# One decoder layer on one core: the opening's modulation rows asked for one block sooner, and the last head's scores and outputs as three float32r products each

## The chip, the cores and the metric

The kernel runs on one core of one Trainium2 chip. The core has five engines with an instruction stream each: TensorE (PE, matrix products; its weight loads are listed as PEld), VectorE (DVE), ScalarE (ACT), GpSimd (POOL) and SyncE (SP), which here only issues transfers between HBM and the on-chip memory SBUF. Matrix products are written into PSUM. The metric is the device time of one execution in microseconds (us); less is better.

## The reference

The reference is one layer of a decoder with 512 positions and a width of 1024, all in float32. A conditioning vector `c` gives six rows of 1024 numbers, the modulation, which scale, shift and gate the two halves of the layer.

```
mod = silu(c) @ ada_w + ada_b                  # 6 rows: sh1, sc1, g1, sh2, sc2, g2
u   = rms_norm(x, mix_pre_g) * (1 + sc1) + sh1
proj = u @ w_in                                # q, k, v, o gate, i/f gates, glu
q, k = silu(causal depthwise conv, width 4)
h   = mlstm(q, k, v, i, f)                     # 4 heads x 256, see below
y   = silu(layer_norm(causal depthwise conv, width 31, of a * sigmoid(gt)))
x   = x + g1 * rms_norm(concat(h, y) @ w_out, mix_post_g)
u   = rms_norm(x, ffn_pre_g) * (1 + sc2) + sh2
a, gt = causal depthwise conv, width 3, of u @ ffn_up
x   = x + g2 * rms_norm((silu(gt) * a) @ ffn_down, ffn_post_g)
```

For each of the four heads the mLSTM amounts to a causal attention without softmax: the scores q·k are multiplied by an exponential weight of the gates, E, and the result is multiplied with v. One more column of ones beside v gives the divisor. The head's output is normalised, gated and goes through `w_out` with the convolution group.

## The kernel before

**Number types.** A float32 product on PE is issued as two instructions. For its large products the kernel uses float32r, a shorter type, and makes up for it by splitting each operand into a high part (the rounded value, written by ACT) and a low part (what is left, subtracted on POOL or DVE). `mm3` (L207) then issues three products, high x high, high x low and low x high, into the same PSUM bank. `w_split` (L185) makes both parts of a weight tile; `w_load` (L195) loads and splits. The attention of all four heads is in plain float32.

**Order.** PE and SP issue in the order in which the text traces the instructions. Within the block `in_order()` (L76) the same holds for DVE, ACT and POOL; elsewhere a scheduler places their instructions when the kernel is built, earlier text first. `behind(ins, anchor)` fixes that one instruction comes after another on its engine. A tile from a pool with n buffers waits until the tile that last had its buffer has been read for good; `slots` has 36 buffers of 128x512 numbers, from which most temporary tiles come. SP is one queue: an issue that waits holds up all behind it.

**The opening** (to L423) loads x, normalises and transposes it, and computes the first three pairs of `glu` columns of `u @ w_in`: a loop over eight blocks k of 128 rows of the width (L352). A block needs

- the modulation row k, 1 MB (`first_load(k)`, L241: two transfers of 512 KB). DVE multiplies it with silu(c) and sums it (`part_sum`, L324) into the block's scale and shift. These rows have four buffers: `raws` for k = 0, 1, 4, 5 and `early_raws` for k = 2, 3, 6, 7;
- the weight row k, 384 KB (`w_rows(k)`, L341), split by ACT and POOL (`w_part`, L345). These rows have two buffers, the pool `adas`, so that row k+2 waits until row k has been split;
- x, scaled and shifted and split: `u[k]`.

PE then runs 18 products of the block into six PSUM banks (`glu_pass`, L348). SP's order before, with m for a modulation row and w for a weight row: m0, a small vector, w0, m1, w1, m2, then per block w2 m3 | w3 m4 and the other vectors | w4 m5 | w5 m6 | w6 m7 | w7, and after these the weights of the next glu columns, which use the buffers of `raws`.

**The middle** computes the projections and the attention head by head. `make_vo(h)` (L490) makes v and the gate of a head in four steps of 128 positions: 24 products, then ACT copies v out of PSUM and forms the gate's tanh. `make_E(h)` (L639) makes the four weight tiles E of a head, which hold 512, 384, 256 and 128 columns, with seven exponentials on ACT. `attention(h)` (L543) is a generator; between its steps PE does other products:

- scores: for each of four tiles two products (the head's 256 rows are two halves), 512, 384, 256 and 128 columns wide; DVE multiplies them into E;
- outputs: for each of four blocks of positions one to four products of E and v, 258 columns wide; ACT takes them out of PSUM;
- then the norm, and after a last step the transposition and the split into `hh` and `hl`.

For the last head (h = 3) the steps lie between the products of `mix_first` (L900 on), which multiply the finished groups by `w_out`: scores 0 and 1, mix 0, scores 2 and 3, mix 1 to 4, outputs 0 and 1, mix 5, output 2, mix 6, output 3, mix 7 to 9, the transposition, mix 10 to 15. `norm_tiles` makes the y group's split tiles meanwhile, 16 of the slots.

**The rest**, the second half of `w_out`, the up projection and the down projection, is a nearly unbroken stream of float32r products on PE.

Of the kernel before, what the change touches and what calls it, by code (L numbers as in the profile page):

```python
# [10 lines left out]
F32 = mybir.dt.float32  # L11
F32R = mybir.dt.float32r
# [43 lines left out]
def decoder_layer(ctx, tc, w_glu0, x, c, adaT, vecs, w_glu, w_qko, w_v0, w_vo, w_out, w_up, w_down, out):  # L56
# [18 lines left out]
    @contextmanager  # L75
    def in_order():  # L76

        traced = nc.cur_bb.bb.instructions
        first = traced[-1]
        yield  # L80
        a = next(i for i in reversed(range(len(traced))) if traced[i] is first) + 1
        last = {}
        for ins in traced[a:]:
            if ins.engine in (V.engine, S.engine, G.engine):
                if ins.engine in last:
                    tc.add_manual_dep(ins, last[ins.engine].name, mybir.DependencyInfo(mybir.DependencyClass.NoSync, mybir.DependencyReason.DATA),
                                      reason="program order")
                last[ins.engine] = ins

    def slot(name, dt=F32):  # L90
        return slots.tile([P, T], dt, tag="t", name=name)
# [149 lines left out]
    def first_load(k):  # L241

        r = (raws if k % 4 < 2 else early_raws).tile([P, 2048], F32, tag="raw", name=f"ada{k}")
        for i in range(2):
            nc.sync.dma_start(r[:, i * D : (i + 1) * D], adaT[k][:, i * D : (i + 1) * D])
        first.append(r)
# [105 lines left out]
    for k in range(KT):  # L352
        wk = []

        if k == 0:
            w_rows(0)
            first_load(1)
        if k + 1 < KT:
            w_rows(k + 1)
        if k + 2 < KT:  # L360
            first_load(k + 2)
        if k == 2:
            nc.sync.dma_start(vec[:, FIRST:], vecs[:, FIRST:])
        hi, lo = u[k]
        if k == 0:
            w_part(k, 0, T)
            part_sum(k, 0)
            part_sum(k, 1)
            part_gains(k)
            sc, sh = parts[k][1][:, :1], parts[k][1][:, 1:]  # L370
            S.activation(hi, xT_ps[0], AF.Identity, scale=sc, bias=sh)
            x_out(1, V)
            x_out(2, S)
            x_out(3, S)
            V.tensor_scalar(out=xr[0], in0=xT_ps[0], scalar1=sc, scalar2=sh, op0=ALU.mult, op1=ALU.add)
            G.tensor_tensor(out=lo, in0=xr[k], in1=hi.bitcast(F32), op=ALU.subtract)
            w_part(k, T, (G0 - 4) * P)
            x_out(4, V)
            x_out(5, S)
            for i, p in ((0, 0), (1, 0), (0, 1), (1, 1), (2, 0), (2, 1), (3, 0), (3, 1)):  # L380
                glu_pass(banks0[i], i, p)
            for j in range(6, KT):
                for tt in range(NT):
                    turn_x(j, tt)
            wk, first_wk = [], wk
            w_part(1, 0, T)
            wk, next_wk = first_wk, wk
            x_out(6, S)
            x_out(7, S)
            for i in range(4):  # L390
                glu_pass(banks0[i], i, 2)
            for p in range(3):
                for i in range(4, G0):
                    glu_pass(banks0[i], i, p)
        else:
            if k == 1:
                wk = next_wk
            else:
                w_part(k, 0, T)
            w_part(k, T, (G0 - 4) * P)  # L400
            part_sum(k, 0)
            part_sum(k, 1)
            part_gains(k)
            sc, sh = parts[k][1][:, :1], parts[k][1][:, 1:]
            S.activation(hi, xr[k], AF.Identity, scale=sc, bias=sh)
            S.activation(xr[k], xr[k], AF.Identity, scale=sc, bias=sh)
            (V if k == KT - 1 else G).tensor_tensor(out=lo, in0=xr[k], in1=hi.bitcast(F32), op=ALU.subtract)
            if k < KT - 1:
                for p in range(3):
                    for i, ps in enumerate(banks0):  # L410
                        glu_pass(ps, i, p)
            else:
                for i, ps in enumerate(banks0):
                    glu_pass(ps, i, 0)
                for i, ps in enumerate(banks0):
                    glu_pass(ps, i, 2)
                    glu_pass(ps, i, 1)
        if k == 6:
            V.tensor_scalar(out=cvw, in0=vcols("cv_dw_w", 0, CK * KT), scalar1=0.5, scalar2=None, op0=ALU.mult)
            V.tensor_scalar(out=ghalf, in0=vcols("ml_norm_g", 0, KT), scalar1=0.5, scalar2=None, op0=ALU.mult)  # L420
# [40 lines left out]
    gz = const.tile([P, NT, 2 * H], F32, name="gz")  # L461
    GB = 2 * H

    def v_tile(h):
        va = vpool.tile([P, 2 * T + 8], F32, tag="vh", name=f"v{h}").rearrange("p (c n) -> p c n", c=NT)

        V.tensor_copy(va[:, :, DH:], ones[:, None, :2].to_broadcast([P, NT, 2]))
        vs[h] = [va[:, cc, :] for cc in range(NT)]
# [18 lines left out]
    def part_of(two, tt):  # L487
        return two[tt // 2][:, (tt % 2) * DH : (tt % 2 + 1) * DH]

    def make_vo(h):  # L490

        w = [z for q in range(2) for z in w_load(w_vo[h - 1, q], f"wvo{h}_{q}")]
        v_tile(h)
        gate = [slot(f"so{h}_{i}") for i in range(2)]
        heads[h][3].extend(gate)
        for tt in range(NT):
            ps = mmbank(f"vo{h}_{tt}")
            ts = slice(tt * P, (tt + 1) * P)
            for k in range(KT):
                mm3(ps, (u[k][0][:, ts], u[k][1][:, ts]), w[k], k == 0, k == KT - 1)  # L500
            S.activation(vs[h][tt][:, :DH], ps[:, :DH], AF.Copy)
            S.activation(part_of(gate, tt), ps[:, DH:], AF.Tanh, scale=0.5)
            yield

    def conv4(ps, i, name):
# [32 lines left out]
            so.append(t)  # L538

    last_lo = [None]  # L540
    last_e = [None]

    def attention(h):  # L543

        _, qs, ks, so = heads[h]

        for cc in range(NT):
            n = NS[cc]
            sp = atbank(f"s{h}_{cc}")
            for d in range(2):  # L550
                PE.matmul(sp[:, :n], ks[d][:, cc * P : (cc + 1) * P], qs[d][:, cc * P :], start=d == 0, stop=d == 1)  # L551
            last_e[0] = V.scalar_tensor_tensor(out=E[h][cc], in0=sp[:, :n], scalar=DH**-0.5, in1=E[h][cc], op0=ALU.mult, op1=ALU.mult)
            if cc in ((0, 2, 3) if h == 0 else (1, 3)):
                yield
        ssq = small.tile([P, NT], F32, tag="ssq", name=f"ssq{h}")
# [2 lines left out]
        for tt in range(NT):  # L558
            o = atbank(f"o{h}_{tt}")
            for cc in range(tt + 1):  # L560
                a = (tt - cc) * P
                PE.matmul(o[:, : DH + 2], E[h][cc][:, a : a + P], vs[h][cc], start=cc == 0, stop=cc == tt)  # L562
            junk = small.tile([P, DH], BF16, tag="junk2", bufs=1, name=f"junko{h}_{tt}")
            hv = hn[tt // 2][:, (tt % 2) * DH : (tt % 2 + 1) * DH]
            S.activation(dm[:, tt : tt + 1], o[:, DH : DH + 1], AF.Abs)
            S.activation(hv, o[:, :DH], AF.Copy)
            S.activation(junk, hv, AF.Square, accum_out=ssq[:, tt : tt + 1])
            if h and tt % 2:
                V.scalar_tensor_tensor(out=hn[tt // 2], in0=so[tt // 2], scalar=1.0, in1=hn[tt // 2], op0=ALU.add, op1=ALU.mult)
            if tt in (1, 2):  # L570
                yield
# [67 lines left out]
    def make_E(h):  # L639
        mb = atbank(f"Mb{h}")  # L640
        PE.matmul(mb, pick[:, h : h + 1].to_broadcast([P, P]), Mhl, start=True, stop=True)
        md = slot(f"Md{h}")
        V.tensor_tensor(out=md.rearrange("p (t m) -> p t m", t=NT), in0=mb.rearrange("p (t m) -> p t m", t=NT),
                        in1=cmask[:, None, :].to_broadcast([P, NT, P]), op=ALU.add)
        E[h] = head_tiles(f"E{h}", F32)
        for cc in range(NT):
            b = ga[:, cc, h : h + 1]
            S.activation(E[h][cc][:, :P], md[:, cc * P : (cc + 1) * P], AF.Exp, bias=b, scale=-1.0)
            if cc < NT - 1:
                S.activation(E[h][cc][:, P:], mb[:, (cc + 1) * P :], AF.Exp, bias=b, scale=-1.0)  # L650
    head_load(0)
    head_proj(0, 0)
    head_proj(0, 1)
# [96 lines left out]
    ys = [None] * KT  # L750
    ysum = const.tile([P, T], F32, name="ysum")
    ysq = const.tile([P, T], F32, name="ysq")

    def behind(ins, anchor):
        tc.add_manual_dep(ins.ins, anchor.ins.name, mybir.DependencyInfo(mybir.DependencyClass.NoSync, mybir.DependencyReason.DATA),
                          reason="order on an engine")

    def conv_tile(j, every=CK):

# [83 lines left out]
    for h in range(H - 1):  # L843
# [37 lines left out]
            pace()  # L881
        make_E(h + 1)
        if h == H - 2:
            norm_mean()
        next(values)
        if h < H - 2:
# [492 lines left out]
```

## Time and profile before

| | us |
|---|---|
| median of 3 runs | 768.74 |
| lowest, highest | 768.34, 769.21 |
| the profiled execution | 769.16 |
| its span in the profile | 767.4 |

The profile is one execution. Its span runs from the first instruction of the program to the end of the last; the 1.76 us between span and time lie around it. In the rows of the timeline the columns are start, length, engine, line, operation, tiles (written, arrow, read), shape and count; in brackets the time for which the engine was idle just before and what ended that. Successive matrix products overlap in the profile, so that the step from one start to the next is the cost of a product, and not the length given. In the rows of the windows the columns are the window, its length, the busy time and count of PE, PEld, DVE, ACT and POOL, then the granted clock of PE as a share of full speed, the mean busy share of the transfer engines and what they moved in GB/s. "SPq" is SP issuing a transfer. Tiles are named as in the text without their numbers: `wglu` is a raw weight row, `wglu_0h` the high part of its first 512 columns, `ada` a modulation row, `s` a score bank, `o` an output bank.

### The profile page before, as it was taken

Reading aid. Unit: us, or ns where it says so; the run is one execution under the profiler, and the core shown is the slowest. Engines: PE = TensorE matmul, PEld = TensorE weight load, DVE = VectorE, ACT = ScalarE, POOL = GpSimd, SP = SyncE. Lnnn points to the kernel's source line nnn. Section 1 sums busy time; section 2 is a strip of 40 time slices with the busy share of each in tenths; the row PEclk is TensorE's granted clock in tenths of the full one; section 3 lists DMA queues with packets and bytes.
Section 4 is the critical chain, followed back from the end, with each engine's and each line's share of the span. In section 5 each row is a group of like instructions: output and inputs, shape, how many; then the busy total and the mean of one; then the engine's idle time right before and its main releaser. Section 6 shows DMA issues by size and latency. Waiting matters only on the chain.

```text
span 767.4 us, 10129 instructions
## 1 busy us (share of the span) xinstructions
PE 756.0 (99%) x3480; PEld 625.1 (81%) x3480; DVE 576.6 (75%) x837; ACT 410.7 (54%) x778; POOL 516.5 (67%) x428
## 2 busy tenths in 40 slices
PE   7999999999999999999999999999999999999996
PEld 5778898878788788888889988888888888888885
DVE  6669999979979696476989978675684775654547
ACT  6675428585665655573345444443534444566633
POOL 4779849796494872645631179786887884599943
PEclk9999999999999999999999999999999999999999
DMA  8973313411131241655965755666767565796273
GB/s 317 349 281 113 112 56 117 158 56 56 55 111 56 98 168 64 235 199 168 365 222 183 271 210 191 240 219 247 262 231 275 187 239 185 271 397 241 93 249 135
DMA packets 40136, 147.32 MB, mean 192 GB/s; under 512 B 3826, under 2 KB 5266, under 8 KB 30484
## 3 DMA queue, kind: packets, MB, share of 16 engines
q1 hardware_dynamic: 27524, 96.59, 34.9%
q10 hardware_dynamic: 12560, 50.08, 18.3%
q8 instruction: 27, 0.44, 0.2%
q14 instruction: 25, 0.20, 0.1%
HBM read 126.59 MB, written 20.07 MB: 191 GB/s over the span
## 4 chain that ended last, share of the span: by engine, by line
PE 93%; DMA 4%; POOL 1%; ACT 1%; issue 0%; DVEq 0%; SPq 0%; DVE 0%; POOLq 0%; ACTq 0%
PE up L210 31%; PE dn L210 13%; PE qko L210 13%; PE vo L210 9%; PE glu L210 7%; PE mixa L210 6%; PE mixb L210 6%; DMA wglu<-in_w_glu 3%; PE o L562 2%; PE s L551 2%; PE v L210 2%; PE glu L350 1%; DMA xn<-in_x 1%; PE xT L992 0%; PE hT L593 0%
## 5 line engine op out<-in xcount | busy, mean ns | idle before, releaser
L774 DVE SCALAR_TENSOR_TENSOR cv<-gt,cvw,cv 128x485 f32<-128x485 f32 (+24 forms) x200 | 137.2, 731 | 2.1 <-ACT cv L762 0.8
L770 POOL TENSOR_TENSOR cs<-cs,cs 128x510 f32<-128x510 f32 (+3 forms) x32 | 42.1, 1316 | 0.2
L192 POOL TENSOR_TENSOR wup_0l<-wup,wup_0h 128x512 fp32r<-128x512 f32 x18 | 25.0, 1389 | 19.4 <-ACT wup_0h L191 19.3
L210 PE MATMUL up<-u2h,wup_0h 128*128 128x512 f32 (+1 forms) x96 | 35.8, 373 | 0.0
L210 PE MATMUL up<-u2h,wup_0l 128*128 128x512 f32 (+1 forms) x96 | 35.7, 371 | 0.0
L210 PE MATMUL up<-u2h,wup_512h 128*128 128x512 f32 (+1 forms) x96 | 35.6, 371 | 0.0
L210 PE MATMUL up<-u2l,wup_512h 128*128 128x512 f32 (+1 forms) x96 | 35.6, 371 | 0.0
L210 PE MATMUL up<-u2h,wup_512l 128*128 128x512 f32 (+1 forms) x96 | 35.6, 371 | 0.0
L210 PE MATMUL up<-u2l,wup_0h 128*128 128x512 f32 (+1 forms) x96 | 35.6, 371 | 0.0
L210 PE MATMUL up<-u2h,wup_1024h 128*128 128x512 f32 (+1 forms) x92 | 35.0, 381 | 0.0
L210 PE MATMUL up<-u2l,wup_1024h 128*128 128x512 f32 (+1 forms) x92 | 34.9, 380 | 0.0
L210 PE MATMUL up<-u2h,wup_1536l 128*128 128x512 f32 (+1 forms) x92 | 34.9, 380 | 0.0
L210 PE MATMUL up<-u2h,wup_1536h 128*128 128x512 f32 (+1 forms) x92 | 34.9, 380 | 0.0
L210 PE MATMUL up<-u2l,wup_1536h 128*128 128x512 f32 (+1 forms) x92 | 34.9, 380 | 0.0
L210 PE MATMUL up<-u2h,wup_1024l 128*128 128x512 f32 (+1 forms) x92 | 34.9, 380 | 0.0
L176 DVE SCALAR_TENSOR_TENSOR junk<-ada,cb 128x1024 bf16<-128x1024 f32 x20 | 29.9, 1493 | 2.6 <-DMA ada<-in_adaT 2.5
L768 ACT ACTIVATE cs<-gt,cvw 128x511 f32<-128x511 f32 (+4 forms) x40 | 27.1, 713 | 6.1 <-POOL cs L770 3.5
L192 POOL TENSOR_TENSOR wup_1536l<-wup,wup_1536h 128x512 fp32r<-128x512 f32 x18 | 24.6, 1365 | 6.0 <-ACT wup_1536h L191 5.4
L191 ACT ACTIVATE wup_512h<-wup 128x512 fp32r<-128x512 f32 x22 | 13.8, 629 | 25.7 <-PE up L210 20.9
L192 POOL TENSOR_TENSOR wup_1024l<-wup,wup_1024h 128x512 fp32r<-128x512 f32 x18 | 23.6, 1314 | 5.0 <-ACT wup_1024h L191 5.0
L330 DVE SCALAR_TENSOR_TENSOR junk<-ada,cps 128x1024 bf16<-128x1024 f32 x16 | 19.5, 1220 | 9.8 <-DMA ada<-in_adaT 9.2
L1113 DVE TENSOR_TENSOR b<-b 128x512 f32<-128x512 f32 x11 | 19.4, 1762 | 8.6 <-POOL b L1112 8.6
(1097 smaller groups left out, 2726.8 us busy)
## 6 DMA issues: line engine op xcount, KB each, us to landing
wup<-in_w_up SPq DMA_DIRECT2D x22, 1024.0 KB, 5.0
b<-in_w_down ACTq DMA_DIRECT2D x11, 1024.0 KB, 5.1
spill_t<-b ACTq DMA_DIRECT2D x11, 1024.0 KB, 3.9
ada<-in_adaT ACTq DMA_DIRECT2D x20, 512.0 KB, 4.8
wqko<-in_w_qko SPq DMA_DIRECT2D x9, 1024.0 KB, 4.8
ada<-in_adaT SPq DMA_DIRECT2D x16, 512.0 KB, 7.5
wo<-in_w_out SPq DMA_DIRECT2D x8, 1024.0 KB, 5.5
wvo<-in_w_vo SPq DMA_DIRECT2D x6, 1024.0 KB, 4.8
```

Source lines behind the costliest of these rows:

```text
L176: t = V.scalar_tensor_tensor(out=junk, in0=r, scalar=1.0, in1=cb, op0=ALU.mult, op1=ALU.mult, accum_out=mod[:, i : i + 1])
L191: S.activation(hi[:, :n], src, AF.Copy)
L192: (eng or G).tensor_tensor(out=lo[:, :n], in0=src, in1=hi[:, :n].bitcast(F32), op=ALU.subtract)
L210: PE.matmul(ps, l, r, start=start and i == 0, stop=stop and i == 2, skip_group_check=again)
L330: V.scalar_tensor_tensor(out=junk, in0=first[k][:, i * D : (i + 1) * D], scalar=1.0, in1=cps, op0=ALU.mult, op1=ALU.mult, accum_out=part[: ...
L350: PE.matmul(ps, blk(wk, i)[a], u[k][b], start=k == 0 and p == 0, stop=k == KT - 1 and p == 1)
L551: PE.matmul(sp[:, :n], ks[d][:, cc * P : (cc + 1) * P], qs[d][:, cc * P :], start=d == 0, stop=d == 1)
L562: PE.matmul(o[:, : DH + 2], E[h][cc][:, a : a + P], vs[h][cc], start=cc == 0, stop=cc == tt)
L768: S.activation(t[:, d:], cvx[j][:, : T - d], AF.Copy, scale=w(CK - 1 - d))
L770: G.tensor_tensor(out=side[:, d:], in0=side[:, d:], in1=t[:, d:], op=ALU.add)
L774: tap = V.scalar_tensor_tensor(out=cp[:, d:], in0=cvx[j][:, : T - d], scalar=w(CK - 1 - d), in1=cp[:, d:], op0=ALU.mult, op1=ALU.add)
L1113: V.tensor_tensor(out=b22, in0=b22, in1=b11, op=ALU.subtract)
```

## The change

There are two edits that do not depend on each other.

**In the opening**, SP's order becomes m0, the small vector, w0, m1, w1, m2, m3, then per block m4 w2 | m5 w3 and the other vectors | m6 w4 | m7 w5 | w6 | w7. Modulation rows are asked for three blocks ahead instead of two, and ahead of the block's weight row instead of after it. Nothing else in the loop is changed.

```diff
         if k == 0:
             w_rows(0)
             first_load(1)
-        if k + 1 < KT:
+        if k == 0:
+            w_rows(1)
+            first_load(2)
+        if k + 3 < KT:
+            first_load(k + 3)
+        if 0 < k < KT - 1:
             w_rows(k + 1)
-        if k + 2 < KT:
-            first_load(k + 2)
```

**In the last head**, q, k, E and v are split into high and low parts, and scores and outputs become three float32r products each. `split_head` splits the two q and two k tiles (four copies on ACT, four subtractions on POOL), with the copies behind the last exponential of the head's E. v is written as float32r by ACT's copy out of PSUM, and DVE subtracts it from PSUM to give a low part, four times 256 columns. Each finished E tile is copied by ACT and subtracted on POOL. Beside the tiles replaced this takes eight slots for q and k, six for E and two for v. The low part of v has no column of ones, so the middle product of three is 256 columns wide and the other two 258.

```diff
@@ v_tile
-        va = vpool.tile([P, 2 * T + 8], F32, tag="vh", ...)
+        va = vpool.tile([P, 2 * T + 8], F32R if h == H - 1 else F32, tag="vh", ...)
@@ make_vo
+            if h == H - 1:
+                if tt % 2 == 0:
+                    vlo.append(slot(f"vl{tt}", F32R))
+                V.tensor_tensor(out=part_of(vlo, tt), in0=ps[:, :DH], in1=vs[h][tt][:, :DH].bitcast(F32), op=ALU.subtract)
@@ new
+    def split_head(h, anchor):
+        for zs in heads[h][1:3]:
+            for i, z in enumerate(zs):
+                hi, lo = slot(f"zh{h}_{i}", F32R), slot(f"zl{h}_{i}", F32R)
+                behind(S.activation(hi, z, AF.Copy), anchor)
+                G.tensor_tensor(out=lo, in0=z, in1=hi.bitcast(F32), op=ALU.subtract)
+                zs[i] = hi, lo
@@ attention
+        if h == H - 1:
+            Eh, El = head_tiles("Eh", F32R), head_tiles("El", F32R)
...
-                PE.matmul(sp[:, :n], ks[d][...], qs[d][...], start=d == 0, stop=d == 1)
+                if h == H - 1:
+                    mm3(sp[:, :n], [z[:, cc * P : (cc + 1) * P] for z in ks[d]], [z[:, cc * P :] for z in qs[d]], d == 0, d == 1)
+                else:
+                    PE.matmul(sp[:, :n], ks[d][...], qs[d][...], start=d == 0, stop=d == 1)
...
+            if h == H - 1:
+                S.activation(Eh[cc], E[h][cc], AF.Copy)
+                G.tensor_tensor(out=El[cc], in0=E[h][cc], in1=Eh[cc].bitcast(F32), op=ALU.subtract)
...
-                PE.matmul(o[:, : DH + 2], E[h][cc][:, a : a + P], vs[h][cc], start=cc == 0, stop=cc == tt)
+                if h < H - 1:
+                    PE.matmul(o[:, : DH + 2], E[h][cc][:, a : a + P], vs[h][cc], start=cc == 0, stop=cc == tt)
+                    continue
+                PE.matmul(o[:, : DH + 2], Eh[cc][:, a : a + P], vs[h][cc], start=cc == 0, stop=False)
+                PE.matmul(o[:, :DH], Eh[cc][:, a : a + P], part_of(vlo, cc), start=False, stop=False)
+                PE.matmul(o[:, : DH + 2], El[cc][:, a : a + P], vs[h][cc], start=False, stop=cc == tt)
@@ after make_E(h + 1), before norm_mean()
         if h == H - 2:
+            split_head(h + 1, last_exp[0])
             norm_mean()
```

`make_E` also keeps its last exponential in `last_exp`, and `behind` moves up in the text.

More of the change, by code (lines that the diff above doesn't have):

```diff
@@ L88, in in_order, with behind @@
                 last[ins.engine] = ins
+    def behind(ins, anchor):
+        tc.add_manual_dep(ins.ins, anchor.ins.name, mybir.DependencyInfo(mybir.DependencyClass.NoSync, mybir.DependencyReason.DATA),
+                          reason="order on an engine")
     def slot(name, dt=F32):
@@ L462, in decoder_layer @@
     GB = 2 * H
+    vlo = []
     def v_tile(h):
-        va = vpool.tile([P, 2 * T + 8], F32, tag="vh", name=f"v{h}").rearrange("p (c n) -> p c n", c=NT)
+        va = vpool.tile([P, 2 * T + 8], F32R if h == H - 1 else F32, tag="vh", name=f"v{h}").rearrange("p (c n) -> p c n", c=NT)
         V.tensor_copy(va[:, :, DH:], ones[:, None, :2].to_broadcast([P, NT, 2]))
@@ L540, in decoder_layer @@
     last_lo = [None]
+    last_exp = [None]
     last_e = [None]
+    def split_head(h, anchor):
[5 more added lines that the diff above has]
+                zs[i] = hi, lo
     def attention(h):
         _, qs, ks, so = heads[h]
+        if h == H - 1:
+            Eh, El = head_tiles("Eh", F32R), head_tiles("El", F32R)
         for cc in range(NT):
@@ L550, in attention @@
             for d in range(2):
-                PE.matmul(sp[:, :n], ks[d][:, cc * P : (cc + 1) * P], qs[d][:, cc * P :], start=d == 0, stop=d == 1)
+                if h == H - 1:
+                    mm3(sp[:, :n], [z[:, cc * P : (cc + 1) * P] for z in ks[d]], [z[:, cc * P :] for z in qs[d]], d == 0, d == 1)
+                else:
+                    PE.matmul(sp[:, :n], ks[d][:, cc * P : (cc + 1) * P], qs[d][:, cc * P :], start=d == 0, stop=d == 1)
             last_e[0] = V.scalar_tensor_tensor(out=E[h][cc], in0=sp[:, :n], scalar=DH**-0.5, in1=E[h][cc], op0=ALU.mult, op1=ALU.mult)
+            if h == H - 1:
+                S.activation(Eh[cc], E[h][cc], AF.Copy)
+                G.tensor_tensor(out=El[cc], in0=E[h][cc], in1=Eh[cc].bitcast(F32), op=ALU.subtract)
             if cc in ((0, 2, 3) if h == 0 else (1, 3)):
@@ L649, in make_E @@
             if cc < NT - 1:
-                S.activation(E[h][cc][:, P:], mb[:, (cc + 1) * P :], AF.Exp, bias=b, scale=-1.0)
+                last_exp[0] = S.activation(E[h][cc][:, P:], mb[:, (cc + 1) * P :], AF.Exp, bias=b, scale=-1.0)
     head_load(0)
@@ L752, in decoder_layer @@
     ysq = const.tile([P, T], F32, name="ysq")
-    def behind(ins, anchor):
-        tc.add_manual_dep(ins.ins, anchor.ins.name, mybir.DependencyInfo(mybir.DependencyClass.NoSync, mybir.DependencyReason.DATA),
-                          reason="order on an engine")
     def conv_tile(j, every=CK):
```

## The prediction

> **What bounds the kernel now.** I read the page first: TensorE (PE) is busy 99% of the span and carries 93% of the chain that ended last. Whatever shortens PE's stream, or makes it wait, moves the end by as much; work of the other engines counts only where PE waits for it.
>
> ```profile
> span 767.4 us, 10129 instructions
> ...
> PE 756.0 (99%) x3480; PEld 625.1 (81%) x3480; DVE 576.6 (75%) x837; ACT 410.7 (54%) x778; POOL 516.5 (67%) x428
> ...
> PE 93%; DMA 4%; POOL 1%; ACT 1%; issue 0%; DVEq 0%; SPq 0%; DVE 0%; POOLq 0%; ACTq 0%
> ```
>
> Then the chain in order of time (start, length, what), and the timelines of the opening.
>
> ```profile
> 34.32 6.28 DMA wglu<-in_w_glu
> ...
> 42.72 8.45 PE glu L350 x36
> ...
> 51.18 54.40 PE glu L210 x240
> ```
>
> The reader is to see that the chain runs over loads of the `wglu` rows until 42.72, and from there over PE alone to 758 us: a shift of the opening's end is carried to the end of the kernel whole. PE's timeline shows how tight the opening is:
>
> ```profile
> 20.67 1.07 PE L350 MATMUL glu<-uh,wglu_0h 128*128 128x512 f32 x4
> ...
> 24.75 1.07 PE L350 MATMUL glu<-uh,wglu_0h 128*128 128x512 f32 x4
> ...
> 29.02 1.21 PE L350 MATMUL glu<-uh,wglu_0h 128*128 128x512 f32 x4
> ...
> 33.29 1.21 PE L350 MATMUL glu<-uh,wglu_0h 128*128 128x512 f32 x4
> ...
> 42.72 1.20 PE L350 MATMUL glu<-uh,wglu_0h 128*128 128x512 f32 x4 [0.94 <-ACT uh L405]
> ```
>
> These are the starts of blocks 1, 2, 3, 4 and 6 of the opening's loop. A block is 18 products and takes 24.75-20.67 = 4.08 us. Blocks 3 and 4 start 0.19 late, block 6 about 1.1 late (33.29+2x4.08 = 41.45, with small gaps counted in); so some 1.5 us is all that an ideal opening could win. What is late there is the weight row, not the modulation row:
>
> ```profile
> 21.80 0.63 ACT L191 ACTIVATE wglu_0h<-wglu 128x512 fp32r<-128x512 f32 x1 [0.71 <-DMA wglu<-in_w_glu]
> ...
> 27.32 0.63 ACT L191 ACTIVATE wglu_0h<-wglu 128x512 fp32r<-128x512 f32 x1 [3.03 <-DMA wglu<-in_w_glu]
> ...
> 35.12 0.63 ACT L191 ACTIVATE wglu_0h<-wglu 128x512 fp32r<-128x512 f32 x1 [1.03 <-DMA wglu<-in_w_glu]
> ...
> 41.03 0.63 ACT L191 ACTIVATE wglu_0h<-wglu 128x512 fp32r<-128x512 f32 x1 [3.41 <-DMA wglu<-in_w_glu]
> ```
>
> ACT stands idle for weight rows 2, 3, 5 and 6, and PE's block begins 29.02-27.32 = 1.70 us after row 3 arrives. The modulation row of block 3 is done earlier: its gains end at 26.55.
>
> ```profile
> 26.35 0.20 DVE L336 TENSOR_SCALAR gsk<-adap,vec 128x1 f32<-128x1 f32 x1
> 28.63 1.22 DVE L330 SCALAR_TENSOR_TENSOR junk<-ada,cps 128x1024 bf16<-128x1024 f32 x1 [2.08 <-DMA ada<-in_adaT]
> ```
>
> **The opening's queue.** All these loads are issued by SP, in the order of the text.
>
> ```profile
> 9.46 2.27 SPq L245 DMA_DIRECT2D ada<-in_adaT  x2
> ...
> 18.18 0.33 SPq L343 DMA_DIRECT2D wglu<-in_w_glu  x1
> 18.55 0.91 SPq L245 DMA_DIRECT2D ada<-in_adaT  x2
> ...
> 20.38 0.33 SPq L343 DMA_DIRECT2D wglu<-in_w_glu  x1
> ```
>
> ```profile
> GB/s 0 96 354 384 391 322 240 400 427 415 401 415 234 282 277 395 418 386 409 390 387 356 310 373 311 236 281 369 388 431 426 391 328 197 30 0 98 393 208 0
> ...
> ada<-in_adaT SPq DMA_DIRECT2D x16, 512.0 KB, 7.5
> wglu<-in_w_glu SPq DMA_DIRECT2D x8, 384.0 KB, 6.7
> ```
>
> SP's timeline first, then the DMA view of 0 to 60 us: 40 slices of 1.5 us, and the sizes. Modulation row 3, weight row 3 and modulation row 4 are issued in this order (18.55, 20.38, and right after) and used in it (done at 26.55, begun at 27.32, begun at 28.63): I take the queue as first in, first out. Before, SP stands from 11.7 to 18.18 at weight row 2, which waits until the buffer of row 0 is free (its low part on POOL); modulation row 3 stands behind it. The queue runs dry meanwhile: the three slices from 18 to 22.5 us move 264 GB/s where the next six move 397. That is 1.5 us of transfer lost.
>
> The change puts modulation row 3 right behind row 2 (issued from 11.7 on) and row 4 ahead of weight row 2. Row 4 needs the buffer of row 0, free at 14.04:
>
> ```profile
> 12.82 1.22 DVE L330 SCALAR_TENSOR_TENSOR junk<-ada,cps 128x1024 bf16<-128x1024 f32 x1
> ```
>
> So SP has sent rows 3 and 4 (four DMAs, 2 MB) before 18.18. Weight row 2 is still not issued before 18.18, when POOL has read row 0, and now it lands behind these 2 MB. The idle gap goes; the late thing is next weight row 2, which before came at 21.80 with 24.75-21.80-1.70 = 1.25 us to spare.
>
> **Working it out by bytes.** Up to weight row 3 the old queue delivered modulation rows 0-3 and weight rows 0-3, at 27.32. Up to weight row 2 the new one delivers modulation rows 0-4 and weight rows 0-2: 1024-384 = 640 KB more, 0.655 MB / 397 GB/s = 1.65 us. Less the gap of 1.5 it arrives at 27.32+1.65-1.5 = 27.47, and block 2 starts at 29.17 instead of 24.75. Six blocks of 4.08 end at 53.65.
> Is a later row worse? Weight row 4 now comes after modulation row 6: again 640 KB more than stood before old row 5 (35.12), so 35.27, block 4 possible at 36.97, due at 37.33: no wait. Row 5 comes behind all modulation rows, 640 KB after old row 6 (41.03), less 1.5 and less the 1.4 lost in the slices from 36 to 40.5 (311, 236, 281): 39.8, block 5 at 41.5, due at 41.4. Rows 6 and 7 follow an empty queue and are early.
> Old end of the opening: six blocks from 24.75 would end at 49.23; they ended about 51.05 (block 6 at 42.72 plus two blocks, with 0.15 of small gaps). **Opening: 53.65-51.05 = +2.6 us.** Bounds: at the best slice, 427 GB/s, everything up to weight row 4 is about 1 us sooner and row 2 with it, and the opening ends near 52.9: +1.9. With none of the gap regained, row 2 comes at 28.97: +4.1.
> Modulation rows being early win nothing: they were no block's last arrival except beside a weight row.
>
> **The last head on PE.** Single widths stand in head 0's scores, all four outputs in the last head's; a wider product of the short type stands in mixa (512 columns), v (264) and up (256).
>
> ```profile
> 157.43 1.72 PE s L551 x4
> ...
> 164.64 2.15 PE s L551 x8
> ...
> 172.24 0.45 PE s L551 x4
> ...
> 105.58 11.52 PE v L210 x96
> ...
> 317.24 2.73 PE mixa L210 x12
> ...
> 333.11 1.31 PE o L562 x6
> ...
> 337.15 1.31 PE o L562 x6
> ...
> 341.20 1.74 PE o L562 x8
> ...
> 414.00 2.87 PE up L210 x24
> ```
>
> A float32 product stands there as two instructions. Scores now: 1.72 (512) + 2.15 (384 and 256) + 0.45 (128) = 4.32 us. Outputs: 1.31+1.31+1.74 = 4.36. Of the short type, 512 columns take 2.73/12 = 0.227, 264 take 11.52/96 = 0.120, 256 take 2.87/24 = 0.120, and between 256 and 512 lies 0.173 for 384 (an estimate on the straight line).
> Outputs after: ten times (258, 256, 258 columns) = 30 x 0.120 = 3.60: -0.76 us.
> Scores after: two halves of the head by three products, 6 x (0.227+0.173+0.120) = 3.12, and 6 products of 128 columns, which no row of the short type shows. Below: on the same line, 0.066 each, 0.40. From the 256 row: 0.120, 0.72. Above: as long as a whole float32 product of that shape, 0.45/2 = 0.225, 1.35. The ends are far apart; nothing shows that the short type keeps its advantage below 256 columns (264 and 256 cost the same, so the line is already broken there), and the only row of this shape is the float32 one. I take 0.225: 3.12+1.35-4.32 = +0.15. **Last head on PE: -0.76+0.15 = -0.6 us**, and -1.24 or -1.56 with the cheaper prices.
> [...]
>
> **What lies beside PE.** Costed at nothing, each with its cover:
>
> ```profile
> 304.41 0.40 ACT L648 ACTIVATE E<-Md,ga 128x128 f32<-128x128 f32 x1
> ...
> 309.46 1.30 POOL L192 TENSOR_TENSOR wo_1024l<-wo,wo_1024h 128x512 fp32r<-128x512 f32 x1 [10.97 <-ACT wo_1024h L191]
> ...
> 313.99 1.10 PE L551 MATMUL s<-q_0c,k_2c 128*128 128x512 f32 x2
> ```
>
> The four q and k tiles are split behind the last exponentials (about 304.8): ACT 4 x 0.63, POOL 4 x 1.30, the last low part near 304.8+0.63+5.2 = 310.6. POOL was idle for 10.97 us there, and the scores start at 313.99: 3.4 us to spare. If that cover is gone (the wo splits put first on POOL: 4 x 1.3 us), PE waits up to 2 us. The score tiles' high and low parts (1280 columns: about 1.6 us of ACT, 3.3 of POOL) are ready before 326; the outputs start at 333. The four low parts of v are DVE reads of 256 columns, well under the 1.22 that 1024 take above, with `mixa`'s banks first needed three microseconds after the last. Of 36 slots the change takes 16 more for a while; the y tiles that could wait for one are used from 352 us on, after the score tiles are free.
>
> **Sum.** +2.6-0.6 = +2.0 us. The profiled execution took 769.16 (span 767.4 and 1.76 around it) and would take 771.2; it lies 0.4 above the median 768.74, on which I put the sum: **770.7**. A measurement of this kernel tells 0.2%, 1.54 us, from no change: beyond 770.3 it is slower.
>
> **The rivals.**
> (1) The opening loses less and the head wins more: opening +1.9, narrow products at 0.066 to 0.120, head -1.2 to -1.6: net +0.3 to +0.7, about 769.3. For it: rates of 400 to 427 in the slices from 10.5 to 18 us. Against: the 2 MB ahead of weight row 2 take 4.9 us by the best rate and 5.3 by the mean, so the rate alone decides little.
> (2) Faster: the transfers are not strictly in issue order, or the 2 MB sent early are through before weight row 2 is issued at 18.18. Then row 2 is on time, no gap is left, and block waits of 1.5 us go: -1.5-0.6 = -2.1, or 766.6. It decides at weight row 2's arrival: before 23.05 (24.75-1.70) the opening wins. Against it: the slices up to 18 us are full without them, so nearly all of the 2 MB is still to come at 18.18, and needs 5.3 us.
> (3) The granted clock falls. PE would stand about 4 us before block 2.
>
> ```profile
> 760.77 0.39 PE L210 MATMUL dn<-p_10h,a_512l 128*128 128x512 f32 x1
> ```
>
> ```profile
> 762.00:764.00 2.00, 0.00 (x0) 0.00 (x0) 1.93 (x4) 0.00 (x0) 0.55 (x1) 1.00 0.58 217
> 764.00:767.00 3.00, 0.00 (x0) 0.00 (x0) 0.27 (x1) 0.00 (x0) 0.00 (x0) 0.74 0.47 175
> ```
>
> At the kernel's end PE's last product starts at 760.77 and it stops at 761.2; in the windows behind, the granted clock (third figure from the right) is full to 764 and 0.74 of full after, which is half speed from about 765.4: 4.2 us of rest were enough. If that happens before block 2, a block or more at half speed adds 2 to 3.5: 773.2. [...]
> (4) The splits of q and k come late and PE waits 1 to 2 us at the first scores: 772.2.
>
> **Chances.** Forecast 0.42 (its own range 769.7 to 772.2, a little of it within 0.2%), (1) 0.26, (2) 0.13, (3) 0.09, (4) 0.10. Slower by over 0.2%: 0.42+0.09+0.10 less 0.05 = 0.56; within: 0.26+0.05 = 0.31; faster 0.13. The range leaves out (2) and the upper part of (3): 768.6 to 773.2.
>
> **What would show it.** Right: SP issues modulation rows 3 and 4 before weight row 2; ACT's first `wglu_0h` of block 2 moves from 21.80 to about 27.5 and PE shows one long wait (about 4 us) before block 2 and hardly any later; the slices from 18 to 22.5 fill up to 400 GB/s; outputs of the last head take 3.6 us; the clock column stays full. Wrong: block 2 near 24.75; 128-column products far under 0.225; a PE wait at 314 or 333.

## The result

| | us |
|---|---|
| before, median of 6 | 768.54 |
| changed, median of 6 | 772.81 (772.23 to 773.73) |
| changed, the profiled execution | 772.23 |
| its span | 770.5 |

The ratio is 1.0057, 95% interval 1.0044 to 1.007: the change costs about 4.3 us by the medians, and 772.23-769.16 = 3.07 us between the two profiled executions, of which the one after is the fastest of its six. The accounts below are made for the profiled pair.

The changed kernel's page says the same of the whole as before; PE, busy 756.2 us (98%), still bounds it.

The waits of PE from 12 us on (total, times, longest) name two new places: block 2 of the opening, and the first product of the gates' cumulative sum, `fcum`.

```profile
PE glu L354 <- ACT uh L412: 3.4, 1, 3.4
...
PE fcum L694 <- DVE g_lf L655: 0.5, 1, 0.5
```

**The opening.** SP's timeline, then the DMA view's slices of 1.5 us, of the changed kernel:

```profile
9.85 5.09 SPq L249 DMA_DIRECT2D ada<-in_adaT  x6
18.24 0.33 SPq L347 DMA_DIRECT2D wglu<-in_w_glu  x1
```

```profile
GB/s 0 63 351 403 333 403 291 401 419 418 407 415 407 404 412 415 395 401 393 418 413 379 315 396 143 109 164 5 206 449 415 426 393 363 112 0 104 350 246 55
```

Modulation rows 2, 3 and 4 go out as six transfers before 15 us, weight row 2 not before 18.24. The slices from 18 to 22.5 us, 264 GB/s before, now read 407, 404 and 412: the gap is filled. But the weight row stands at the end of it. ACT's first use of weight rows 2 and 3:

```profile
26.71 0.63 ACT L195 ACTIVATE wglu_0h<-wglu 128x512 fp32r<-128x512 f32 x1 [5.57 <-DMA wglu<-in_w_glu]
...
30.21 0.63 ACT L195 ACTIVATE wglu_0h<-wglu 128x512 fp32r<-128x512 f32 x1 [1.02 <-DMA wglu<-in_w_glu]
```

Row 2 comes at 26.71 instead of 21.80; row 3 behind it is in time. PE's timeline, the starts of blocks 2, 3 and 4 and the second piece of block 2, and PE's windows around them:

```profile
28.40 2.07 PE L354 MATMUL glu<-uh,wglu_0h 128*128 128x512 f32 x4 [3.44 <-ACT uh L412]
30.27 1.05 PE L354 MATMUL glu<-uh,wglu_512h 128*128 128x512 f32 x2
...
34.16 1.07 PE L354 MATMUL glu<-uh,wglu_0h 128*128 128x512 f32 x4
...
38.23 1.07 PE L354 MATMUL glu<-uh,wglu_0h 128*128 128x512 f32 x4
```

```profile
24.70:28.00 3.30, 0.26 (x2) 0.00 (x0) 2.88 (x9) 1.29 (x3) 0.58 (x1) 1.00 1.02 402
28.00:30.00 2.00, 1.60 (x4) 1.31 (x5) 1.88 (x3) 1.16 (x2) 2.00 (x3) 0.59 1.04 409
30.00:32.00 2.00, 2.00 (x7) 1.57 (x6) 0.83 (x4) 1.75 (x4) 1.70 (x2) 0.56 1.02 405
32.00:36.00 4.00, 4.00 (x20) 3.30 (x19) 3.64 (x8) 2.27 (x4) 3.01 (x4) 1.00 1.00 361
```

Block 3 begins 34.16-28.40 = 5.76 us after block 2; block 4 begins 4.07 after block 3. The first four products of block 2 take 30.27-28.40 = 1.87, double the usual 0.91. The granted clock says why: 0.59 and 0.56 from 28 to 32 us, 1.00 before and after; by half microseconds it reads 0.50 from 28.5 to 31.5. That is half speed for some 3.4 us, and it costs 5.76-4.08 = 1.68.

The sum of the opening: block 2 starts 28.40-24.75 = 3.65 later; the slow clock adds 1.68; the 1.8 us of waits that blocks 3 to 7 had before are gone. Its end moves by +3.53 us, from 51.02 to 54.55, where PE's timelines have the first product of the next projection (51.18 and 54.72 in the chains).

**The gates.** Chain of before, then of the changed kernel:

```profile
127.98 0.79 PE fcum L658 x8
```

```profile
54.72 54.40 PE glu L214 x240
...
132.00 1.05 PE fcum L694 x8
...
133.05 11.01 PE qko L214 x48
```

`qko` went on at 128.77 before (127.98+0.79) and at 133.05 now, 4.28 later instead of 3.53: another 0.75 us is lost here, far from both edits.

**The last head.** The scores in the chain of before:

```profile
314.13 3.12 PE s L551 x8
...
319.98 1.31 PE s L551 x8
```

The chain of the changed kernel, with the mixes between to bound the outputs, and from its timeline the first product of 128 columns and the one behind the last:

```profile
318.38 2.56 PE s L214 x12
320.93 2.76 PE mixa L214 x12
323.70 1.33 PE s L214 x12
...
336.86 0.12 PE o L596
...
337.96 2.74 PE mixa L214 x12
340.70 0.12 PE o L596
...
341.79 2.73 PE mixa L214 x12
344.52 0.12 PE o L596
...
345.98 8.23 PE mixa L214 x36
```

```profile
324.25 0.22 PE L214 MATMUL s<-zh,zh 128*128 128x128 f32 x1
...
324.87 1.11 PE L227 MATMUL ry_b<-ident,ry_r 128*128 128x128 f32 x8
```

Scores: 2.56+1.33 = 3.89 us, 3.12+1.31 = 4.43 in the same places before. Outputs, each from its first product to the next mix: 1.10+1.09+1.46 = 3.65, 4.36 before. No wait stands before either. Of the 1.33 us, six products of 256 columns take 0.72 (0.120 each); the six of 128 columns take the other 0.61 or 0.62, 0.10 each on the mean and 0.11 from one start to the next behind the first. Together -1.25 us, and 3.53+0.75-1.25 = 3.0 of the 3.07 are accounted for.

### The profile page after: what moved, and what is told of

It is laid out like the page before. It is cut to its first block, busy times and chain, and to the rows that moved or that the text cites. A ratio compares the mean times of both kernels' runs of the same rounds, so it can differ in the third digit from the quotient of the medians.

```text
span 770.5 us, 10196 instructions
## 1 busy us (share of the span) xinstructions
PE 756.2 (98%) x3498; PEld 627.1 (81%) x3498; DVE 582.9 (76%) x841; ACT 414.1 (54%) x786; POOL 529.3 (69%) x436
## 4 chain that ended last, share of the span: by engine, by line
PE 93%; DMA 2%; DVE 1%; ACT 1%; issue 1%; POOL 0%; DVEq 0%; POOLq 0%; SPq 0%; ACTq 0%
PE up L214 31%; PE dn L214 13%; PE qko L214 11%; PE vo L214 9%; PE glu L214 7%; PE mixa L214 6%; PE mixb L214 6%; PE glu L354 3%; PE o L594 2%; PE s L579 2%; PE v L214 1%; DMA wglu<-in_w_glu 1%; DMA xn<-in_x 1%; PE s L214 1%; PE xT L1025 0%
## 5 line engine op out<-in xcount | busy, mean ns | idle before, releaser
L806 DVE SCALAR_TENSOR_TENSOR cv<-gt,cvw,cv 128x485 f32<-128x485 f32 (+23 forms) x200 | 137.2, 730 | 2.2 <-ACT cv L794 0.8
L195 ACT ACTIVATE wup_512h<-wup 128x512 fp32r<-128x512 f32 x22 | 13.8, 629 | 27.3 <-PE up L214 22.4
L196 POOL TENSOR_TENSOR wup_512l<-wup,wup_512h 128x512 fp32r<-128x512 f32 x18 | 24.2, 1347 | 1.2 <-ACT wup_512h L195 1.2
```

The lines of the kernel that those rows point to most:

```text
L195: S.activation(hi[:, :n], src, AF.Copy)
L196: (eng or G).tensor_tensor(out=lo[:, :n], in0=src, in1=hi[:, :n].bitcast(F32), op=ALU.subtract)
L806: tap = V.scalar_tensor_tensor(out=cp[:, d:], in0=cvx[j][:, : T - d], scalar=w(CK - 1 - d), in1=cp[:, d:], op0=ALU.mult, op1=ALU.add)
```

## The experiments

Each experiment was run in turns with the kernel before on one chip, in two sets: `open_only`, `heads_only`, `busy` and `half_heads` on one chip, the others on another. Ratios are to the kernel before of the same set, with 95% intervals.

### The two edits apart

`open_only` is the kernel before with the first diff of the change alone.

> The change's opening with the heads of before. Theory (the loss sits in the opening alone: weight row 2 waits behind 2 MB of modulation rows, and the granted clock falls while PE waits): weight row 2 is first used near 26.7 us, PE waits 3.4 us before block 2, block 2 takes about 5.8 us instead of 4.1, the opening ends 3.5 us later than before, and the time is 3.5 to 5.5 us over that of before. Rival (a part of the loss comes from the last head's new tiles and copies): at most 2.6 us over before.

Measured: 774.00 us, ratio 1.0067 (1.0047 to 1.0087). PE's timeline and windows of `open_only`:

```profile
28.00 1.20 PE L350 MATMUL glu<-uh,wglu_0h 128*128 128x512 f32 x4 [1.92 <-ACT uh L408]
...
33.83 0.84 PE L350 MATMUL glu<-uh,wglu_0h 128*128 128x512 f32 x3
```

```profile
28.00:29.10 1.10, 1.09 (x5) 0.92 (x6) 1.10 (x5) 0.80 (x1) 1.10 (x3) 1.00 1.05 413
29.10:32.50 3.40, 3.40 (x10) 2.63 (x9) 2.32 (x7) 2.08 (x4) 2.54 (x3) 0.50 1.03 409
```

Block 2 takes 5.83 us here too. In this execution PE's block 1 began 1.1 us later (21.84), row 2 came no later (26.31), so PE rested only 1.92 us; the clock still halved, 1.1 us after PE had resumed. The 3.4 us rest that the expectation named was not needed. The time is 5.3 us over before, the upper end of the expectation, and the wait at `fcum` is there as well (0.5 us), so it belongs to the opening's edit. The rival, a loss in the last head, falls.

`heads_only` is the changed kernel with the opening of before.

> The opening of before with the change's last head. Theory: PE's scores take 3.9 us instead of 4.4 and its outputs 3.65 instead of 4.36, no new wait, the time is 1.2 us under that of before (ratio 0.998). Rival (the new tiles hold slots and engines and cost a wait, as the 0.5 us wait at fcum in the changed kernel could mean): the time is that of before or more.

Measured: 767.66 us, ratio 0.9985 (0.9965 to 1.0004). The chain of `heads_only` has

```profile
313.72 2.56 PE s L214 x12
...
319.04 1.33 PE s L214 x12
```

the scores of the changed kernel, and no wait at `fcum`. By the medians it gains 1.0 us where 1.2 were expected; the interval reaches just past 1, so the gain is shown by the rows and only made likely by the times.

### The clock

`busy` is the changed kernel with products that add nothing, where PE waits (`none` is a tile of zeros; its two lines are left out):

```diff
+            if k == 2:
+                for _ in range(14):
+                    PE.matmul(banks0[0], none, u[0][0], start=False, stop=False)
             if k < KT - 1:
                 for p in range(3):
```

> The changed kernel with 14 products of zero weights, added into a bank without changing it, between block 1 and block 2 of the opening, where PE waits for weight row 2; 3.2 us of PE. [...] Rival (block 2 is slow because of what it reads or because the queue is full): block 2 still takes 5.8 us and the time is that of the changed kernel.

Measured: 771.03 us (770.24 to 771.79), ratio 1.0027 (1.0008 to 1.0046). PE's timeline and windows of `busy`:

```profile
24.12 3.33 PE L419 MATMUL glu<-uh,none 128*128 128x512 f32 x14
28.43 1.20 PE L356 MATMUL glu<-uh,wglu_0h 128*128 128x512 f32 x4 [0.98 <-ACT uh L414]
...
32.67 1.07 PE L356 MATMUL glu<-uh,wglu_0h 128*128 128x512 f32 x4
```

```profile
28.00:32.00 4.00, 3.56 (x16) 2.93 (x17) 2.77 (x6) 2.88 (x6) 3.69 (x4) 1.00 1.03 408
```

Block 2 starts as late as before, at 28.43, with the queue as full (408 GB/s), and takes 4.24 us where it took 5.76. The clock column is full (1.00). So the slow block came from PE's rest, not from what it read: shown. The time is 1.8 us under the 772.81 of the changed kernel, which ran in another set (by the ratios it is 2.3 us). Not all of it is the clock: `fcum` isn't waited for in this kernel either, as told below. The runs do not lie closer together: 1.55 us from the lowest to the highest, 1.5 in the six of the changed kernel.

`after_again` is the changed kernel unchanged.

> The changed kernel once more, for a second profile of it and for times beside the next three. [...] Rival (one chance drop in the one profile): block 2 takes 4.1 us and the clock column is full.

Measured: 772.83 us (772.22 to 774.11), ratio 1.0054 (1.004 to 1.0067). Its second profile has a rest of 4.2 us, a block 2 of 34.80-28.99 = 5.81 us and a wait of 0.4 at `fcum`. With `open_only` and `pin` below that makes four profiles of this opening, and all four have the slow clock at block 2. The runs' times go with their mean clock only in part: the two lowest clocks (0.993) belong to 773.73 and 773.76, but the slowest run, 774.11, had 0.997. In `open_only` they go together: the five runs at 0.994 and 0.995 are the five slowest (774.92 to 775.93). A mean clock also counts the fall behind PE's last product, which costs nothing and differs from run to run: in `pin` the column reads 0.50 from 766 us on, in `after_again` it is full up to 770. The rest of the spread stays open.

The length of the rest alone doesn't set the moment of the fall. Worked out from the clock column of one-microsecond windows, taking the low clock as 0.50, it comes at block 2 3.4, 3.0, 4.7 and 4.0 us after PE's last product before the rest (the result's profile, `open_only`, `after_again`, `pin`), and at the kernel's end between 2.2 us (`pin`) and 5.3 us (`after_again`) after PE's last product of all, over all ten profiles.

### The wait at fcum

The scheduler that orders DVE, ACT and POOL when the kernel is built is the planner of this text. `pin` is the changed kernel with two orders fixed; `gate_abs` and `gate_lf` name the first and the last step of the gates:

```diff
+            if (h, part) == (0, 1):
+                behind(last_split[0], gate_abs)
...
+            if name == "q0_0" and d == 1:
+                behind(last_e[0], gate_lf)
```

> The changed kernel with two orders fixed in the gates' stretch: on ACT the copy of the last piece of the second qko weight comes after the gates' first step, and on DVE the first tap of q's convolution comes after the gates' last step. Theory (PE's 0.5 us wait at fcum comes from the order that the planner chose once the opening was longer): no wait at fcum, the distance from the opening's end to fcum falls from 77.45 to 76.8 us, the time is about 0.65 us under the changed kernel. Rival (another engine's work is later by itself): the wait stays.

Measured: 771.86 us, ratio 1.0039 (1.0026 to 1.0051); beside `after_again`, in the same turns, 1.0 us less. The two intervals overlap, so the gain is shown by the rows below, and the times agree with it. PE's waits of `pin` from 12 us on:

```profile
PE glu L356 <- ACT uh L414: 3.9, 1, 3.9
PE glu L356 <- ACT uh L380: 0.8, 1, 0.8
```

The wait at `fcum` is gone, and `fcum` follows the opening's end after 131.54-54.73 = 76.8 us, as before the change (127.82-51.02), and not 132.00-54.55 = 77.45 as in the changed kernel. On DVE's timelines (kernel before, then changed kernel) one sees what the planner had done:

```profile
126.41 0.70 DVE L619 SCALAR_TENSOR_TENSOR g_lf<-gz,g_fl 128x16 f32<-128x16 f32 x1
127.03 0.74 DVE L511 SCALAR_TENSOR_TENSOR q_0c<-qko,vec,q_0c 128x511 f32<-128x511 f32 x1
```

```profile
129.37 0.74 DVE L524 SCALAR_TENSOR_TENSOR q_0c<-qko,vec,q_0c 128x511 f32<-128x511 f32 x1
...
130.65 1.29 DVE L655 SCALAR_TENSOR_TENSOR g_lf<-gz,g_fl 128x16 f32<-128x16 f32 x1
```

Before, `g_lf`, which PE waits for, comes ahead of the first tap of q (the first step of its convolution); after, it comes behind it. Of the two orders that `pin` fixes, DVE's is the one that counts: ACT's step of the gates that DVE waits for, `g_fe`, starts 68.7 us after the opening's end in the kernel before, the changed kernel and `pin` alike. The tap's place alone doesn't decide, though. In `busy` `g_lf` stands behind the tap too, at 127.94, but with five steps of the `cv` convolution ahead of it in the gates' stretch instead of six; it starts 74.9 us after the opening's end (76.1 in the changed kernel, 75.4 before) and PE doesn't wait. What the wait depends on is how much other work DVE has been given between the gates' steps.

That order was never written down in the text of the kernel; outside `in_order` it is the planner's. `open_only` shows that the opening's edit alone changes it, with the tap at 129.07 and `g_lf` at 130.36. Why the planner decided so, most likely by its picture of the times, no run here shows.

### How far ahead

`one_ahead` has the heads of before and the change's opening, in which it keeps the modulation row in front of the weight row but takes back the extra block (its edit against `open_only`):

```diff
         if k == 0:
             w_rows(1)
             first_load(2)
-        if k + 3 < KT:
-            first_load(k + 3)
-        if 0 < k < KT - 1:
-            w_rows(k + 1)
+        else:
+            if k + 2 < KT:
+                first_load(k + 2)
+            if k + 1 < KT:
+                w_rows(k + 1)
```

> The heads of before; in the opening each modulation row k+2 is issued ahead of weight row k+1, as in the change, but not one block sooner: row 4 comes after weight row 2 again. Theory (weight row 2 arrives when all bytes ahead of it have passed; 1 MB less is 2.6 us less): weight row 2 is first used near 24.1 us instead of 26.7, block 2 starts near 25.8, PE waits about 1 us there, the clock stays full, and the opening ends near 50.3, 0.7 us before that of before: 768.0. Rival (being ahead of the weight row is what costs, or the weight rows wait for something else): block 2 starts at 27 or later and the time is 2 us or more over before.

Measured: 768.76 us, ratio 1.0006 (0.9997 to 1.0015). Weight rows 2 to 5 are first used by ACT, in `one_ahead`, at

```profile
22.99 0.63 ACT L191 ACTIVATE wglu_0h<-wglu 128x512 fp32r<-128x512 f32 x1 [2.39 <-DMA wglu<-in_w_glu]
...
27.73 0.63 ACT L191 ACTIVATE wglu_0h<-wglu 128x512 fp32r<-128x512 f32 x1 [2.25 <-DMA wglu<-in_w_glu]
...
32.03 0.63 ACT L191 ACTIVATE wglu_0h<-wglu 128x512 fp32r<-128x512 f32 x1 [1.81 <-DMA wglu<-in_w_glu]
...
36.12 0.63 ACT L191 ACTIVATE wglu_0h<-wglu 128x512 fp32r<-128x512 f32 x1 [1.59 <-DMA wglu<-in_w_glu]
```

The rival falls: with 1 MB less ahead of it, weight row 2 comes 3.7 us sooner than in the changed kernel, more than the 2.6 expected, and almost in time. Of the 3.7 us, 0.55 is that SP issued it earlier in this execution (17.69 instead of 18.24). The clock stays full (0.999 over the profiled execution). But the gain of 0.7 us isn't there: rows 3, 4 and 5 come 0.4, 0.4 and 1.0 us later than before the change (row 4 at 31.59 there), although PE's block 1 had begun 0.5 us earlier. Each of them now has one more modulation row ahead of it in the queue, and by the order of the issues that spends what the filled gap had won. My expectation had looked at row 2 alone.

### Only as much as fits

`half_heads` has the change's last head, and in the opening it puts only the first half of modulation row 3, 512 KB, ahead of weight row 2; all else is in the order of before (its edit against the changed kernel; the part that lets `first_load` issue one half is left out):

```diff
         if k == 0:
             w_rows(1)
             first_load(2)
-        if k + 3 < KT:
-            first_load(k + 3)
-        if 0 < k < KT - 1:
-            w_rows(k + 1)
+            first_load(3, (0,))
+        elif k + 1 < KT:
+            w_rows(k + 1)
+        if k == 1:
+            first_load(3, (1,))
+        elif 1 < k < KT - 2:
+            first_load(k + 2)
```

> The change's last head, and in the opening the order of before except that the first half of modulation row 3 (512 KB) is issued ahead of weight row 2. Theory (the queue is first in, first out and ran dry at 18 us; what it can carry until weight row 2 is issued is free): weight row 2 is first used by 23.1 us, block 2 starts at 24.8, all later rows come about 1.3 us sooner, the opening ends at 49.5 to 50.0 instead of 51.0, and with the last head's 1.2 us the time is about 2.3 us under before (766.2). Rival (a transfer issued ahead of weight row 2 delays it by its whole length however short): block 2 starts at 25.5 or later and the time is 0.5 to 1.2 us under before.

Measured: 766.96 us, ratio 0.9974 (0.9955 to 0.9993). ACT's first uses of rows 2 and 3 and PE's block 2, in `half_heads`:

```profile
22.01 0.63 ACT L195 ACTIVATE wglu_0h<-wglu 128x512 fp32r<-128x512 f32 x1 [1.11 <-DMA wglu<-in_w_glu]
...
25.75 0.63 ACT L195 ACTIVATE wglu_0h<-wglu 128x512 fp32r<-128x512 f32 x1 [1.24 <-DMA wglu<-in_w_glu]
```

```profile
24.54 1.07 PE L355 MATMUL glu<-uh,wglu_0h 128*128 128x512 f32 x4
...
28.62 1.07 PE L355 MATMUL glu<-uh,wglu_0h 128*128 128x512 f32 x4
```

Row 2 is in time, row 3 comes 1.6 us sooner than before, and blocks 2 and 3 start without a wait. The opening ends at 49.87 us instead of 51.02, inside the range expected; 0.2 of that is an earlier start of block 1 (20.46 instead of 20.67). The time falls by 1.7 us instead of 2.3. It is 0.7 us under `heads_only` of the same set, within the intervals: that the opening gains is shown by the rows and only made likely by the times.

`half_wide` is `half_heads` with the last head's narrowest score tile in plain float32 again (`split_head` also keeps the whole tile `z` for it; that line is left out):

```diff
+                if h == H - 1 and cc == NT - 1:
+                    PE.matmul(sp[:, :n], ks[d][2][:, cc * P : (cc + 1) * P], qs[d][2][:, cc * P :], start=d == 0, stop=d == 1)
-                if h == H - 1:
+                elif h == H - 1:
```

> half_heads with the last head's narrowest score tile (128 columns) left as two plain float32 products. In the changed kernel a float32r product of 128 columns took 0.107 us, six of them 0.64, and two float32 ones take 0.45. Theory: scores take 0.2 us less than in half_heads, nothing else moves, the time is that of half_heads less 0.2 (766.8). Rival (the whole q and k tiles, held longer in four slots, make later tiles wait): PE waits at the outputs or at the y products and the time is 0.5 us or more over half_heads.

Measured: 766.14 us, ratio 0.9962 (0.9949 to 0.9974). Its chain has

```profile
317.92 0.71 PE s L214 x6
318.63 0.45 PE s L581 x4
```

1.16 us for the last two score tiles instead of 1.33, and no new wait. The expectation's 0.107 us for a narrow product was a little high; six took 0.61 or 0.62, not 0.64, so 0.10 each. The 0.17 us won is too little to be told apart from `half_heads` by the times; the interval of `half_wide` is clear of 1. It is the fastest version here, 2.5 us under the kernel before.

## Why the prediction was right in sign, and where it was off

**The mechanism held.** The one forecast that carried it, weight row 2 behind 2 MB of modulation rows, is what happened: the gap of the queue filled, row 2 became the last arrival, later blocks had no wait of their own. `open_only` shows that the loss is there, and `one_ahead` that it is the block of lead that makes it, not the row's place in front.

**The sum did not hold**, and that the time still came near it is partly luck. The result, 772.81 us, lies above the forecast's own range (769.7 to 772.2) and inside the whole range only because that took in a part of rival (3). Two losses were not in the sum, the clock (1.68) and the gates (0.75); against them the arrival (0.75) and the head (0.65) came out better than forecast.

**The arrival** was forecast at 27.47 and came at 26.71. About half of the difference is bytes: up to the first use of row 2 the queue had moved 26.7 us x 351 GB/s = 9.37 MB, against 27.3 x 325 = 8.87 up to row 3 before, so 0.50 MB more where I had counted 0.655. The rest is that the queue was fuller than I had taken it: 408 GB/s from 18 to 22.5 us where I had used 397, and 325 instead of 320 up to 18 us. Without the clock the opening would have cost 3.53-1.68 = 1.85 us, the lower bound of the range I gave for it (+1.9).

**The clock** was rival (3), with a chance of 0.09, and it was the wrong side to leave it on: all four profiles of this opening have it, and the full clock column that I had named as a sign of being right did not come. I had priced it at 2 to 3.5 us, for a block or more at half speed, a length that was my estimate and that no row of before shows; it lasted 3.4 us and cost 1.7. The step that failed is the reading of the kernel's end, "4.2 us of rest were enough", as if about that much were needed. In `open_only` 1.92 us were enough, and there too the half speed lasted 3.4 us.

**The narrow product** was the mis-sized term of the head: priced at 0.225 us, half of what the two float32 products of its shape take, it took 0.10. So the head gained 1.25 us and not 0.6; this too I had named as a sign of being wrong. The nearest row was the one of the same type at 256 columns (0.120), not the one of the same shape. That the head came within a hundredth of the -1.24 forecast with 0.12 is luck: the narrow products were 0.1 us cheaper in all, the wide scores 0.16 dearer (2.56 instead of 2.40), and the scores before 4.43 instead of 4.32. The outputs, 30 products at 0.120 for 3.60 us, held (3.65).

**What lies beside PE** held: no wait at the scores or outputs, so rival (4) falls, and with it the worry about the 36 slots.

**Missing from the sum** was 0.75 us at `fcum`. The step "a shift of the opening's end is carried to the end of the kernel whole" failed there: the shift came with another order of DVE's work, which nobody had touched in the text. `pin` shows that the wait goes when that order is fixed.

Forecast terms, +2.6-0.6 = +2.0; measured in the profiled pair, +1.85 (arrival) +1.68 (clock) +0.75 (gates) -1.25 (head) = +3.0. The medians differ by 1.2 us more than the profiled pair, whose one execution lies 0.6 above its median and whose other lies 0.6 below; what sets a single execution's place in the spread stays open.

## What to carry to other kernels

A load asked for sooner is not free because it fills an idle queue: count the bytes that it puts ahead of the next load that somebody waits for, and send only as much as passes before that load can be issued (here the opening ended about 1 us sooner with 512 KB, and 3.5 us later with 2 MB, 1.7 of it the clock). Where PE will stand, price the slow clock behind it too: here it came behind the four rests of 1.92, 3.4, 3.9 and 4.2 us ahead of block 2, and cost 1.7 us in the changed kernel. And when a planner places part of the work, an edit in one stage can change the order in another, so compare the order of the engines there before looking for a cause in the hardware.

## What the runs showed of the hardware that was not expected

A rest of PE of 1.92 us halved the granted clock for the next 3.4 us, starting 1.1 us after PE had resumed (`open_only`). Shorter ones did not: 1.37 us ahead of block 0 in the same execution, 1.31 there and 0.94 at block 6 in the kernel before, 0.98 in `busy`. Nor did the 2.85 us from the start of the span to PE's first product in the kernel before, where the clock column reads 1.00 through the first 20 us. Between 1.37 and 1.92 us nothing was measured, and since the fall came anywhere from 2.2 to 5.3 us after PE's last product, the one rest that was enough gives no threshold.

A float32r product of 128 columns took 0.10 to 0.11 us, nearly as long as one of 256 columns (0.120), so that three of them are slower than one float32 product of the same shape (0.225).
